# Computing five of six modulation sublayers of a two-block transformer kernel on VectorE instead of TensorE

## The chip, the core and the metric

The kernel runs on one core of a Trainium2 chip. The metric is the device time of one launch in microseconds (us). The core has a matrix engine (TensorE, PE in the profile, with its weight loads as PEld), three engines for elementwise work (VectorE, DVE; ScalarE, ACT; GpSimd, POOL), and a queue that issues most transfers (SyncE, SP). Each engine works through its own instructions in order and waits for the others by semaphores.

## The reference, cut to what matters

Two blocks follow one another, each with two layers, on 256 tokens of 1024 channels in float32. The first block has four branches. The second has, in each layer, three sublayers: a feed-forward network (FFN), an attention, a second FFN. Each sublayer normalises its rows and modulates them, by a shift, a scale and a gate that come from two conditioning vectors and one large matrix per layer:

```python
c_act = jax.nn.silu(c)
cc_act = jax.nn.silu(c_ctx)
for layer in range(DEPTH):
    mod = (c_act @ w_mod[layer] + b_mod[layer]).reshape(b, 1, N_MOD, D_MODEL)
    mod_c = (cc_act @ w_mod[layer] + b_mod[layer]).reshape(N_MOD, D_MODEL)
    ...
    shift, scale, gate = mods_of(m, sub)
    y = swiglu(modulate(rms_norm(h, g_pre[sub]), shift, scale), w1, w2)
    return h + MACARON_WEIGHT * gate * rms_norm(y, g_post[sub])
```

`w_mod` is 1024 x 9216 a layer: 3072 columns for each of the 2 x 3 sublayers. Only two rows are multiplied with it.

## The kernel before, in words

All large products are float32 products in three passes. A load (`wload`) brings 1024 columns of weights (128 x 1024, 512 KB) into a buffer `wr` (four of them); ScalarE writes the high part `wh` (L177), VectorE the low part `wl` (L178), three buffers each; TensorE then multiplies high by high, high by low and low by high (L169). In the FFNs and in the attention's projections one load feeds 24 matmuls of 512 columns, alternately into the PSUM banks `ac` and `rw`.

Every `wload` ends with `tick()`, which takes a step of the generators in `self.bg`. So small chains of work are spread between the large products. The modulation is such a generator, `mods`. Its step loads one `wr` tile of `w_mod` and issues two matmuls into the bank `md`, with the conditioning vectors as the stationary part (32 columns wide, so that a product fills one of four column groups of the array). Four steps make a half row; then ScalarE copies `md` out (L1173), two transfers bring it to DRAM, and after six half rows the sums are made, written to DRAM and read back (L1175 to L1199). A sublayer takes 24 steps with products and 9 others. Sublayer (0,0) is made in layer 1 of the first block, a step a tick; the other five run in the second block, a step every second tick (`MODS_TICKS`). `pre`, which opens the next sublayer, waits for its modulation.

Inside the attention, `scores` makes the softmax of two heads (scores in `ac` and `rw`, then VectorE L1529 to L1536, ScalarE, VectorE L1552) and `values` transposes the result and multiplies it with v. There are no weight loads there, so ticks are called by hand: `HEAD_TICKS` = 6 at a pair of heads of the first stream and 2 of the second. `HEADS_AHEAD` = (0, 1) says how many pairs may have their values still to come. A scheduler then sets the final order of the instructions on each engine.

Of the kernel before, what the change touches and what calls it, by code (L numbers as in the profile page):

```python
# [9 lines left out]
F32 = mybir.dt.float32  # L10
# [3 lines left out]
AF = mybir.ActivationFunctionType  # L14
# [5 lines left out]
L = 2  # L20
D = 1024
# [31 lines left out]
RWKV_STEPS = ((2, 1), (2, 1))           # by layer and duo  # L53
RWKV_GAPS = (2, 3, 3, 2, 1, 4)
CONV_STEPS, CONV_GAP, XQ_GAP, MLA_GAPS = 3, 2, 1, (2, 1)
MODS_TICKS = 2                          # ticks a step
HEAD_TICKS = (6, 2)                     # ticks at a pair of heads, by stream
HEADS_AHEAD = (0, 1)                    # pairs whose values wait, by stream
EVS = 5                                 # buffers
COLS = ((0, 1), (1, 2), (3, 2), (5, 2), (7, 1))     # row tiles that are transposed at a time  # L60
# [99 lines left out]
class Build:  # L160
# [6 lines left out]
    # -- building stones --  # L167
# [6 lines left out]
    def split(self, h, l, src, eng=None):  # L174
        """src = h + l exactly, h and l with the 12 significant bits of float32r"""
        nc = self.nc
        nc.scalar.copy(h, src)  # L177
        (eng or nc.vector).tensor_tensor(out=l, in0=src, in1=h.bitcast(F32), op=ALU.subtract)  # L178
# [15 lines left out]
    def gemm(self, out, sa, sb, KT):  # L194
        """out = sum over k of a^T b, three float32r passes; sa(k), sb(k) give (high, low)"""
# [7 lines left out]
    def rsqrt(self, out, in_, n):  # L203
        """out = in_ ** -0.5 (exact to float32 rounding), [p, n]"""
        p = in_.shape[0]
        self.nc.gpsimd.tensor_tensor(out=out, in0=in_, in1=self.mhalf[:p, :n], op=ALU.pow)  # L206
# [9 lines left out]
    def tick(self):  # L216
        """a step of the work that is spread over the stream of weights"""
# [17 lines left out]
    # -- the whole --  # L235
    def build(self):
        nc, tc, ap = self.nc, self.tc, self.ap
        with ExitStack() as st:
# [15 lines left out]
            # what the end of the first block needs on the one side, the rest of it and then the second on the other  # L254
# [7 lines left out]
    # ================= first block =================  # L262
    def first(self, fin, st):
# [3 lines left out]
        self.ts = fin.enter_context(tc.tile_pool(name="ts", bufs=4))     # a few columns  # L267
        p1 = self.p1 = pool("p1", 1)
        self.f4 = fin.enter_context(tc.tile_pool(name="f4", bufs=7))     # [128, 1024]
# [9 lines left out]
        self.t1 = pool("t1", 2)     # [128, 256] scratch  # L279
        self.t2 = pool("t2", 2)     # [128, 512] scratch  # L280
        self.d2 = pool("d2", 16)    # [128, 512], four heads of the recurrence
        self.d4 = pool("d4", 5)     # [128, 1024]
        self.rp = pool("rp", 1)     # its diagonal blocks
# [5 lines left out]
    def trig(self):  # L289
        """cos and sin of positions * inv_freq, [token, tile, 16]"""  # L290
# [27 lines left out]
        # the quotient may be off by one either way  # L318
# [63 lines left out]
    def params(self, l):  # L382
        """the small weights of a layer"""
# [4 lines left out]
        # halves and the like, worked out on the chip  # L388
# [21 lines left out]
    def wtile(self, ps):  # L410
        """the next 128 columns of w_in"""
# [8 lines left out]
    def move(self, ps, h, lo, kt, k0, K, lhs, n=512):  # L420
        """ps += rows k0.. of the weights (n columns each), streamed; lhs(k) the stationary parts"""
# [7 lines left out]
    def memkv(self, l):  # L429
        """k^T [d, head, m] and v [m, (head d)] of the memory tokens"""  # L430
# [29 lines left out]
    def gated(self, n):  # L460
        """silu(gate) times the branch, in two parts: the operands of the output projection"""
# [16 lines left out]
    # -- RWKV --  # L478
    def shift(self, p, mu, omu, out):
        """out = (1 - mu) * p + mu * p_prev, tokens along the free dimension"""  # L480
# [47 lines left out]
        # decay and learning rate  # L528
# [26 lines left out]
        # kk = k * k_k, normalised per head  # L555
# [24 lines left out]
        # scaled operands  # L580
# [18 lines left out]
        # inverses of the 16x16 diagonal blocks, row after row: a row of a block goes to the partitions of its block  # L599
# [26 lines left out]
        # by token  # L626
# [15 lines left out]
        # bonus  # L642
# [12 lines left out]
        # blocks of 32, then of 64  # L655
# [29 lines left out]
        # u = ta S + c0 for the state S of a chunk, and S' = e (m S + cs)  # L685
# [46 lines left out]
        # the rows: rk v + rb u, and r S  # L732
# [9 lines left out]
        # there is no state before the first chunk  # L742
# [19 lines left out]
        # group norm over a head, and the bonus  # L762
# [27 lines left out]
    # -- convolution --  # L790
# [31 lines left out]
    def norm_stats(self, src, eps, n=1):  # L822
        """mean and (variance + eps) ** -0.5 of the rows; src a list of [128, <=512]"""
# [11 lines left out]
    def conv_norm(self):  # L835
        """layer norm over the channels, then silu: self.cx becomes 2 silu(.)"""
# [24 lines left out]
    # -- attention over the memory --  # L861
# [835 lines left out]
```

## Time and profile before

| what | us |
|---|---|
| median of three runs (2756.73, 2757.94, 2766.02) | 2757.94 |
| profiled execution, span from first to last instruction | 2758.4 |
| PE busy in it | 2691.4 |
| DVE busy | 1539.3 |
| ACT busy | 1145.3 |
| POOL busy | 219.5 |

The profiled execution is known by its span; nothing else of it is recorded, and the span stands 0.46 us above the median of the runs. The second block begins at about 868 us of the span. Its stages are, in order: FFN and attention of layer 0, FFN, FFN of layer 1 (from about 1990), attention (from about 2385), last FFN. The two stretches in which the attention makes its scores and values are 1413.5 to 1511 and 2454.5 to 2511; the text calls them the score stages.

### The profile page before, as it was taken

The numbers are of one execution on the slowest core, as the hardware profiler recorded it, in microseconds if no ns is written. First come the engines' busy times: TensorE is split into PE (matmuls) and PEld (weight loads), VectorE is DVE, ScalarE is ACT, GpSimd is POOL, SyncE is SP. The second block draws the span as 40 slices with busy tenths as digits, with TensorE's granted clock in tenths as the row PEclk, the third lists the DMA queues.
The fourth block names the chain that finished last, engine by engine and source line by source line (L and its number), as shares of the span: only waits on it lengthen the run. The fifth ranks groups of instructions, "written<-read, shape, count | busy, mean of one in ns | idle before, by whom it ended". The sixth has DMA issues, their size and how long they took to land.

```text
span 2758.4 us, 43028 instructions
## 1 busy us (share of the span) xinstructions
PE 2691.4 (98%) x17138; PEld 2183.3 (79%) x17138; DVE 1539.3 (56%) x2646; ACT 1145.3 (42%) x1964; POOL 219.5 (8%) x240
## 2 busy tenths in 40 slices
PE   8999999999999999999999999999999999999999
PEld 7888998787999777777755777777777777765897
DVE  7997667897666533345635442335533334744656
ACT  5465455445545322234436422224422224535445
POOL 1121110112011000000102000000000000110000
PEclk9999999999999999999999999999999999999999
DMA  6344466546366534434433344444444343434565
GB/s 204 95 129 131 150 199 212 161 141 183 116 185 204 168 119 130 128 111 127 120 108 111 115 119 127 124 121 118 123 130 122 117 131 116 131 123 135 168 183 151
DMA packets 134906, 385.07 MB, mean 140 GB/s; under 512 B 38481, under 2 KB 42385, under 8 KB 134577
## 3 DMA queue, kind: packets, MB, share of 16 engines
q1 hardware_dynamic: 121216, 379.25, 45.7%
q10 hardware_dynamic: 13488, 3.07, 0.5%
q8 instruction: 135, 2.21, 0.3%
q14 instruction: 67, 0.54, 0.1%
HBM read 379.43 MB, written 2.83 MB: 139 GB/s over the span
## 4 chain that ended last, share of the span: by engine, by line
PE 86%; DVE 8%; ACT 2%; issue 2%; DMA 1%; POOL 1%; ACTq 0%; DVEq 0%; SPq 0%; POOLq 0%
PE ac L169 42%; PE rw L169 27%; PE sm L169 10%; PE md L169 5%; PE sm L172 2%; DVE wl L178 2%; DVE br L817 2%; DMA wr<-in_win 1%; DVE br L1352 0%; ACT wh L177 0%; PE rw L172 0%; POOL rso L206 0%; POOL rs L206 0%; DVE u L1345 0%; DVE u L1263 0%
## 5 line engine op out<-in xcount | busy, mean ns | idle before, releaser
L178 DVE TENSOR_TENSOR wl<-wr,wh 128x1024 fp32r<-128x1024 f32 (+2 forms) x547 | 699.5, 1280 | 507.9 <-ACT wh L177 506.1
L177 ACT CAST wh<-wr 128x1024 fp32r<-128x1024 f32 (+2 forms) x547 | 568.2, 1039 | 953.6 <-PE ac L169 439.2
L169 PE MATMUL rw<-blk,wh 128*128 128x512 f32 (+1 forms) x1712 | 461.6, 354 | 1.3 <-DVE blk L1282 1.1
L169 PE MATMUL ac<-blk,wh 128*128 128x512 f32 (+1 forms) x1728 | 460.8, 352 | 0.0
L169 PE MATMUL ac<-xth,wh 128*128 128x256 f32 x1248 | 357.7, 287 | 5.7 <-ACT wh L177 5.2
L169 PEld LDWEIGHTS rw<-blk,wh 128*128 128x128 f32 x1712 | 302.4, 191 | 71.2 <-ACT wh L177 27.7
L169 PEld LDWEIGHTS ac<-blk,wh 128*128 128x128 f32 x1728 | 305.4, 190 | 58.5 <-ACT wh L177 14.3
L169 PE MATMUL ac<-xth,wl 128*128 128x256 f32 x1248 | 350.0, 281 | 1.2 <-DVE wl L178 1.2
L169 PE MATMUL ac<-xtl,wh 128*128 128x256 f32 x1248 | 349.9, 281 | 0.1
L169 PE MATMUL rw<-blk,wl 128*128 128x512 f32 (+1 forms) x856 | 301.0, 352 | 4.2 <-DVE wl L178 4.2
L169 PE MATMUL ac<-blk,wl 128*128 128x512 f32 (+1 forms) x864 | 301.9, 349 | 1.8 <-DVE wl L178 1.8
L169 PEld LDWEIGHTS ac<-xth,wh 128*128 128x128 f32 x1248 | 236.2, 189 | 22.2 <-issue 10.7
L169 PEld LDWEIGHTS ac<-xth,wl 128*128 128x128 f32 x1248 | 236.1, 189 | 3.8 <-DVE wl L178 2.2
L169 PEld LDWEIGHTS ac<-xtl,wh 128*128 128x128 f32 x1248 | 236.4, 190 | 2.5 <-issue 1.6
L178 DVE TENSOR_TENSOR al<-blk,ah 128x512 fp32r<-128x512 f32 (+1 forms) x170 | 104.9, 621 | 146.8 <-ACT ah L177 146.6
L169 PEld LDWEIGHTS rw<-blk,wl 128*128 128x128 f32 x856 | 163.1, 191 | 26.8 <-DVE wl L178 4.4
L169 PEld LDWEIGHTS ac<-blk,wl 128*128 128x128 f32 x864 | 164.1, 190 | 23.4 <-DVE wl L178 2.2
L177 ACT CAST ah<-blk 128x512 fp32r<-128x512 f32 (+1 forms) x170 | 95.4, 564 | 201.1 <-PE rw L169 102.6
L169 PE MATMUL md<-wr,cs 128*32 128x512 f32 x576 | 158.0, 612 | 3.7 <-DMA wr<-in_wmod 2.2
L1396 DVE SCALAR_TENSOR_TENSOR blk<-u,rw 128x512 f32<-128x512 f32 (+1 forms) x66 | 39.5, 598 | 160.9 <-PE rw L169 160.8
L206 POOL TENSOR_TENSOR rso<-rso,mhalf 128x1 f32<-128x1 f32 x20 | 11.0, 551 | 1420.7 <-DVE rso L1347 1420.7
L169 PE MATMUL ac<-f,wh 128*128 128x256 f32 x640 | 117.0, 282 | 0.0
(417 smaller groups left out, 4112.1 us busy)
## 6 DMA issues: line engine op xcount, KB each, us to landing
wr<-in_w SPq DMA_DIRECT2D x264, 512.0 KB
wr<-in_win SPq DMA_DIRECT2D x187, 512.0 KB
wr<-in_wmod SPq DMA_DIRECT2D x144, 512.0 KB
wr<-in_wo SPq DMA_DIRECT2D x32, 512.0 KB
wr<-in_wout SPq DMA_DIRECT2D x32, 512.0 KB
wr<-in_wkv SPq DMA_DIRECT2D x16, 512.0 KB
gate<-gd SPq DMA_DIRECT2D x10, 512.0 KB
blk<-in_rpb SPq DMA_DIRECT2D x48, 64.0 KB
```

The costliest lines, as they stand in the source:

```text
L169: self.nc.tensor.matmul(out, a, b, start=start, stop=stop, skip_group_check=True)
L172: self.nc.tensor.transpose(out, a, self.ident[:n, :n])
L177: nc.scalar.copy(h, src)
L178: (eng or nc.vector).tensor_tensor(out=l, in0=src, in1=h.bitcast(F32), op=ALU.subtract)
L206: self.nc.gpsimd.tensor_tensor(out=out, in0=in_, in1=self.mhalf[:p, :n], op=ALU.pow)
L817: V.scalar_tensor_tensor(out=acc, in0=hp[:, j : j + 256], scalar=w(j), in1=acc, op0=ALU.mult, op1=ALU.add)
L1396: V.scalar_tensor_tensor(out=a(u // 2), in0=t, scalar=0.5, in1=pu, op0=ALU.mult, op1=ALU.mult)
```

## The change

The modulation of the five sublayers after the first is computed by VectorE. `wmodT` holds the transposed matrix: a tile has 128 output channels in its partitions and the 1024 inputs along them. `cr` holds silu of the two conditioning vectors, copied to all partitions. One instruction per tile and vector (`tensor_tensor_reduce`, L1188, "ISA" in the order, with a second one that reads the accumulator) multiplies and sums. A group of 128 channels is one tile and two such products (one where the second vector isn't needed): 120 groups, 208 products. The group's next tile is fetched after its products; the gaps between groups are 2, 2 and 1 ticks, a step a tick. Shift and scale then lie by channel without a way through DRAM; the gate is transposed once and written to DRAM.

The ticks by hand in the attention go, and `HEADS_AHEAD` becomes (1, 1). Sublayer (0,0) still uses `mods`, but now loads two tiles in one step and issues their four matmuls, one to each column group, in the next. `kernel` sets a smaller DMA scratch, and `second` calls `c_rows`. Comments are left out of the diff.

```diff
-MODS_TICKS = 2                          # ticks a step
-HEAD_TICKS = (6, 2)                     # ticks at a pair of heads, by stream
-HEADS_AHEAD = (0, 1)                    # pairs whose values wait, by stream
+MODS_GAPS = (2, 2, 1)
+HEADS_AHEAD = (1, 1)
...
+    def c_rows(self):
+        nc = self.nc
+        self.cr = self.p2.tile([128, 2, 1024], F32, name="cr")
+        self.prod = self.p2.tile([128, 1024], F32, name="prod")
+        for r in range(2):
+            nc.sync.dma_start(out=self.cr[:, r], in_=self.ap["cR"][r].partition_broadcast(128))
+            nc.scalar.activation(self.prod, self.cr[:, r], AF.Tanh, scale=0.5)
+            nc.vector.scalar_tensor_tensor(out=self.cr[:, r], in0=self.prod, scalar=1.0, in1=self.cr[:, r], op0=ALU.add,
+                                           op1=ALU.mult)
+            nc.vector.tensor_scalar(out=self.cr[:, r], in0=self.cr[:, r], scalar1=0.5, scalar2=None, op0=ALU.mult)
+    def mods_rows(self, *which):
...
+        todo = [(l, sub, g) for l, sub in which for g in range(24)]
+        raw = fetch(*todo[0])
+        yield
+        for n, (l, sub, g) in enumerate(todo):
...
+            for r in range(2 if both(g) else 1):
+                V.tensor_tensor_reduce(out=self.prod, in0=raw, in1=self.cr[:, r], scale=1.0, scalar=0.0, op0=ALU.mult,
+                                       op1=ALU.add, accum_out=m[:, g, r : r + 1])
+            if n + 1 < len(todo):
+                raw = fetch(*todo[n + 1])
...
+            for _ in range(MODS_GAPS[n % len(MODS_GAPS)]):
+                yield
...
     def mods(self, *which):
-                for i in range(4):
+                for i in range(0, 4, 2):
                     u = 4 * blk + i
-                    raw = self.wr.tile([128, 1024], F32, name="wr")
-                    nc.sync.dma_start(out=raw, in_=ap["wmod"][l, :, 1024 * u : 1024 * u + 1024])
-                    for k in range(2):
-                        kk = 2 * i + k
-                        g = 32 * (kk % 4)
-                        self.mm(ps[g : g + 32], self.cs[:, kk], raw[:, 512 * k : 512 * k + 512], kk < 4, kk >= 4)
+                    raw = [self.wr.tile([128, 1024], F32, name="wr") for _ in range(2)]
+                    for j in range(2):
+                        nc.sync.dma_start(out=raw[j], in_=ap["wmod"][l, :, 1024 * (u + j) : 1024 * (u + j) + 1024])
+                    yield
+                    for k in range(4):
+                        self.mm(ps[32 * k : 32 * k + 32], self.cs[:, 2 * i + k],
+                                raw[k // 2][:, 512 * (k % 2) : 512 * (k % 2) + 512], i == 0, i == 2)
                     yield
...
             if l == 0:
-                self.bg.append((self.mods((0, 1), (0, 2), (1, 0), (1, 1), (1, 2)), -MODS_TICKS))
+                self.c_rows()
+                self.bg.append((self.mods_rows((0, 1), (0, 2), (1, 0), (1, 1), (1, 2)), 1))
...
                     P = self.scores(s, kind, heads, q, k, nab, sink)
-                    for _ in range(HEAD_TICKS[s]):
-                        self.tick()
...
-    nc = _bacc.Bacc("TRN2", target_bir_lowering=False, num_devices=1)
+    nc = _bacc.Bacc("TRN2", target_bir_lowering=False, num_devices=1, dynamic_dma_scratch_size=1024)
```

What this does to the order shows best at three places. First TensorE at the start of the score stage of layer 0 (`rw`, `ac` with two `blk`: scores; `ident`: transposes; `md`: modulation). Before:

```order
L169 MATMUL rw_14839<-blk_14046,blk_14047 128x512 x2
L169 MATMUL ac_14840<-blk_14046,blk_14047 128x512 x2
L169 MATMUL md_14863<-wr_14864,cs_6333 32x512 x2
L169 MATMUL md_14863<-wr_14868,cs_6333 32x512 x2
L169 MATMUL md_14863<-wr_14913,cs_6333 32x512 x2
L169 MATMUL md_14863<-wr_14917,cs_6333 32x512 x2
L169 MATMUL rw_14872<-blk_14046,blk_14047 128x512 x2
L169 MATMUL ac_14873<-blk_14046,blk_14047 128x512 x2
```

And in the change:

```order
L168 MATMUL rw_14888<-blk_14083,blk_14084 128x512 x2
L168 MATMUL ac_14889<-blk_14083,blk_14084 128x512 x2
L171 MATMUL md_15792<-ident_69,gt_14835 16x128
L168 MATMUL rw_14908<-blk_14083,blk_14084 128x512 x2
L168 MATMUL ac_14909<-blk_14083,blk_14084 128x512 x2
```

The products of the modulation are gone; one transpose of the gate is left, and the scores follow one another.

Second, VectorE in the first product of layer 0's FFN (`wl`: low parts of the next weights; the two lines with `u2`: the activation; `prod`: the new products). Before:

```order
L178 TENSOR_TENSOR wl_11891<-wr_11888,wh_11890 128x1024
L178 TENSOR_TENSOR wl_11922<-wr_11919,wh_11921 128x1024
L1395 SCALAR_TENSOR_TENSOR u2_11884<-u2_11884,ac_11823 128x512
L1396 SCALAR_TENSOR_TENSOR blk_11347<-u2_11884,rw_11859 128x512
L178 TENSOR_TENSOR wl_11961<-wr_11958,wh_11960 128x1024
```

And in the change:

```order
L177 TENSOR_TENSOR wl_11940<-wr_11937,wh_11939 128x1024
L1455 SCALAR_TENSOR_TENSOR u2_11902<-u2_11902,ac_11842 128x512
L1188 ISA prod_11348,mm_11374<-wr_12015,cr_11347 128x1024
L1188 ISA mm_11374 128x1
L1188 ISA prod_11348,mm_11374<-wr_12015,cr_11347 128x1024
L1188 ISA mm_11374 128x1
L1456 SCALAR_TENSOR_TENSOR blk_11357<-u2_11902,rw_11877 128x512
L177 TENSOR_TENSOR wl_11979<-wr_11976,wh_11978 128x1024
```

The products stand between the low parts of the weights, so a late product makes the next `wl` late.

Third, SyncE's queue at the start of the second block's first FFN (`w1`: weights; `cb`: constants, 1248 KB; `cR`: the conditioning rows, `gate`: the gate rows, 512 KB each). Before:

```order
L185 DMA wr_11607<-in_w1 128x1024
L185 DMA wr_11638<-in_w1 128x1024
L1221 DMA cb_11345<-in_cb 128x2496
L1166 DMA wr_11644<-in_wmod 128x1024
L1292 DMA gate_13011<-gd00_6342 128x1024 x2
L185 DMA wr_11677<-in_w1 128x1024
```

And in the change:

```order
L184 DMA wr_11583<-in_w1 128x1024
L1173 DMA wr_11591<-in_wmodT 128x1024
L1280 DMA cb_11345<-in_cb 128x2496
L1160 DMA cr_11347<-in_cR 128x1024 x2
L1352 DMA gate_13048<-gd00_6342 128x1024 x2
L184 DMA wr_11622<-in_w1 128x1024
```

Before, the weights of the fifth and sixth unit (11607 and 11638) went ahead of `cb`. Now those of the fifth (11622) come after `cb`, the new rows and the gate.

## Rows read from the trace of the kernel before

**Rows 1.** The page: busy time of each engine, share of the span, instructions.

```profile
PE 2691.4 (98%) x17138; PEld 2183.3 (79%) x17138; DVE 1539.3 (56%) x2646; ACT 1145.3 (42%) x1964; POOL 219.5 (8%) x240
```

**Rows 2.** The page: chain that ended last, its shares by engine and line.

```profile
PE ac L169 42%; PE rw L169 27%; PE sm L169 10%; PE md L169 5%; PE sm L172 2%; DVE wl L178 2%; DVE br L817 2%; DMA wr<-in_win 1%; DVE br L1352 0%; ACT wh L177 0%; PE rw L172 0%; POOL rso L206 0%; POOL rs L206 0%; DVE u L1345 0%; DVE u L1263 0%
```

**Rows 3.** That chain in order of time, FFN of layer 0: start, duration, what.

```profile
948.92 5.44 PE ac L169 x24
954.36 0.98 PE md L169 x4
955.34 5.67 PE rw L169 x24
...
1020.27 5.44 PE ac L169 x24
1025.71 5.44 PE rw L169 x24
```

**Rows 4.** Windows, tile md alone: stretch, length; PE, PEld, DVE, ACT; clock, DMA.

```profile
505.00:700.00 195.00, 27.58 (x97) 3.85 (x97) 0.19 (x1) 3.52 (x6) 1.00 0.54 163
868.00:1413.50 545.50, 34.95 (x129) 4.87 (x129) 0.19 (x1) 4.63 (x8) 0.99 0.43 130
1413.50:1511.00 97.50, 17.77 (x73) 2.61 (x73) 0.19 (x1) 2.36 (x4) 0.93 0.39 119
1511.00:2454.50 943.50, 63.48 (x226) 8.86 (x226) 0.39 (x2) 8.13 (x14) 1.00 0.41 122
2454.50:2511.00 56.50, 15.43 (x56) 1.97 (x56) 0.00 (x0) 1.78 (x3) 0.94 0.36 113
```

**Rows 5.** Windows, all work: PE, PEld, DVE, ACT, POOL busy (records); clock, DMA, GB/s.

```profile
511.00:630.00 119.00, 116.83 (x1216) 90.68 (x1214) 110.82 (x255) 49.35 (x100) 19.73 (x24) 1.00 0.51 156
925.00:1190.00 265.00, 265.00 (x1172) 204.44 (x1171) 92.74 (x105) 67.10 (x83) 0.00 (x0) 1.00 0.42 124
1190.00:1330.00 140.00, 138.68 (x673) 108.65 (x671) 74.77 (x107) 62.38 (x108) 9.87 (x9) 1.00 0.42 122
1413.50:1511.00 97.50, 94.96 (x441) 45.74 (x441) 56.08 (x225) 53.29 (x146) 19.40 (x15) 0.93 0.39 119
1850.00:1990.00 140.00, 138.49 (x672) 109.33 (x671) 74.47 (x111) 62.05 (x107) 5.25 (x8) 1.00 0.40 115
2240.00:2385.00 145.00, 143.69 (x685) 113.11 (x684) 75.10 (x113) 63.25 (x110) 5.35 (x9) 1.00 0.42 116
2454.50:2511.00 56.50, 54.14 (x235) 21.44 (x236) 32.00 (x140) 27.34 (x72) 8.31 (x5) 0.94 0.36 113
```

**Rows 6.** Timeline of PE in layer 0's score stage: start, us, instruction.

```profile
1436.10 1.06 PE L169 MATMUL md<-wr,cs 128*32 128x512 f32 x8
1437.10 0.65 PE L169 MATMUL sm<-pt,gate 128*64 128x256 f32 x4
```

**Rows 7.** VectorE's groups by line and shape: busy, mean ns | idle before.

```profile
L178 DVE TENSOR_TENSOR wl<-wr,wh 128x1024 fp32r<-128x1024 f32 x535 | 691.2, 1293 | 501.7 <-ACT wh L177 499.9
L1529 DVE DVE_READ_ACCUMULATOR2_ANT hm<- 128x1 f32 x48 | 6.7, 139 | 0.0
L1529 DVE CUSTOM_DVE_ANT_0 ac<-ac,blk 128x256 f32<-128x256 f32 x12 | 5.1, 426 | 26.0 <-PE ac L169 26.0
L1120 DVE SCALAR_TENSOR_TENSOR br<-br,mvar,d 128x1024 f32<-128x1024 f32 x2 | 2.5, 1274 | 0.0
```

**Rows 8.** What PE waited for from 2335 to 2400: total, times, longest.

```profile
PE rw L169 <- DVE wl L178: 4.2, 1, 4.2
```

**Rows 9.** SyncE's timeline and the windows, 917 to 930.

```profile
917.45 0.33 SPq L1221 DMA_DIRECT2D cb<-in_cb  x1
...
920.00:930.00 10.00, 9.35 (x76) 9.01 (x76) 6.78 (x14) 6.34 (x11) 0.00 (x0) 1.00 0.66 240
```

**Rows 10.** The chain in order of time: fifth unit's matmuls; a weight load.

```profile
936.83 5.44 PE ac L169 x24
...
647.47 5.45 DMA wr<-in_win
```

More of the change, by code (lines that the diff above doesn't have):

```diff
@@ new lines, in mods_rows, with fetch @@
+    def mods_rows(self, *which):
+        nc, ap = self.nc, self.ap
+        V = nc.vector
+        def fetch(l, sub, g):
+            raw = self.wr.tile([128, 1024], F32, name="wr")
+            nc.sync.dma_start(out=raw, in_=ap["wmodT"][l, sub, :, 1024 * g : 1024 * g + 1024])
+            return raw
+        todo = [(l, sub, g) for l, sub in which for g in range(24)]
+        raw = fetch(*todo[0])
+        yield
+        for n, (l, sub, g) in enumerate(todo):
+            if g == 0:
+                both = (lambda g: l < L - 1 or sub == 0 or (sub == 1 and g < 16))
+                m = self.us.tile([128, 24, 2], F32, name="mm", bufs=2)
+                pm = self.us.tile([128, 40], F32, name="pm", bufs=2)
+                nc.sync.dma_start(out=pm, in_=ap["pmodT"][l, sub])
+                nc.gpsimd.memset(m, 0.0)
+            for r in range(2 if both(g) else 1):
[3 more added lines that the diff above has]
+                raw = fetch(*todo[n + 1])
+            if g == 23:
+                col = lambda a: pm[:, a : a + 8].unsqueeze(2).to_broadcast([128, 8, 2])
+                mc = self.mc[l]
+                V.tensor_tensor(out=m, in0=m, in1=pm[:, 0:24].unsqueeze(2).to_broadcast([128, 24, 2]), op=ALU.add)
+                V.tensor_copy(mc[:, 2 * sub], m[:, 0:8])
+                V.scalar_tensor_tensor(out=mc[:, 2 * sub + 1], in0=m[:, 8:16], scalar=1.0, in1=col(24), op0=ALU.add,
+                                       op1=ALU.mult)
+                gt = self.us.tile([128, 2, 8], F32, name="gt", bufs=2)
+                V.scalar_tensor_tensor(out=gt.rearrange("p r k -> p k r"), in0=m[:, 16:24],
+                                       scalar=D**0.5 * (1.0 if sub == 1 else 0.5), in1=col(32), op0=ALU.mult, op1=ALU.mult)
+                yield
+                ps = self.md.tile([128, 512], F32, name="md")
+                self.tr(ps[:16, 0:128], gt.rearrange("p r k -> p (r k)"))
+                gr = self.us.tile([16, 128], F32, name="gr", bufs=2)
+                V.tensor_copy(gr, ps[:16, 0:128])
+                nc.scalar.dma_start(out=self.gd[l, sub][2].rearrange("r (k c) -> (r k) c", c=128), in_=gr)
+                self.modded.add((l, sub))
+            for _ in range(MODS_GAPS[n % len(MODS_GAPS)]):
+                yield
@@ L1162, in mods @@
                 ps = self.md.tile([128, 512], F32, name="md")
-                for i in range(4):
+                for i in range(0, 4, 2):
                     u = 4 * blk + i
-                    raw = self.wr.tile([128, 1024], F32, name="wr")
-                    nc.sync.dma_start(out=raw, in_=ap["wmod"][l, :, 1024 * u : 1024 * u + 1024])
-                    for k in range(2):
-                        kk = 2 * i + k
-                        g = 32 * (kk % 4)
-                        self.mm(ps[g : g + 32], self.cs[:, kk], raw[:, 512 * k : 512 * k + 512], kk < 4, kk >= 4)
+                    raw = [self.wr.tile([128, 1024], F32, name="wr") for _ in range(2)]
+                    for j in range(2):
+                        nc.sync.dma_start(out=raw[j], in_=ap["wmod"][l, :, 1024 * (u + j) : 1024 * (u + j) + 1024])
+                    yield
+                    for k in range(4):
+                        self.mm(ps[32 * k : 32 * k + 32], self.cs[:, 2 * i + k],
+                                raw[k // 2][:, 512 * (k % 2) : 512 * (k % 2) + 512], i == 0, i == 2)
                     yield
@@ L1653, in pack @@
     out["cT"] = np.stack([i["c_2"].reshape(8, 128).T, i["c_ctx_2"].reshape(8, 128).T], 2)
-    out["wmod"] = np.stack([_move(i["w_mod_2"][l], 2) for l in range(L)])
+    out["cR"] = np.stack([i["c_2"].reshape(D), i["c_ctx_2"].reshape(D)])
+    out["wmod"] = _move(i["w_mod_2"][0][:, : 3 * D], 2)[None]
+    out["wmodT"] = i["w_mod_2"].transpose(0, 2, 1).reshape(L, 3, 24, 128, D).transpose(0, 1, 3, 2, 4).reshape(L, 3, 128, -1)
+    cols = [i["b_mod_2"].reshape(L, 3, 24, 128)] + [i[n].reshape(L, 3, 8, 128) for n in ("g_pre_2", "g_post_2")]
+    out["pmodT"] = np.concatenate(cols, 2).transpose(0, 1, 3, 2)
     rows = [i["b_mod_2"].reshape(L, 3, 3, 64, 16)] + [i[n].reshape(L, 3, 1, 64, 16) for n in ("g_pre_2", "g_post_2")]
```

## Prediction

> **What bounds the kernel now.** I read the busy times first: TensorE is busy 98% of the span, VectorE 56%, ScalarE 42% [rows 1]. The chain of work that ended last says the same: most of it is matmuls, and 5% of the span is the modulation's, on the path itself [rows 2]. So time that leaves TensorE is gained, as long as nothing else ends later in its place. The question is what the modulation's matmuls take out of TensorE's time, and whether VectorE, which takes the work over, has room where it gets it.
>
> How dear a step is shows in the chain in order of time [rows 3]. In the FFN a unit of 24 matmuls takes 5.44 us when the next follows at once. Where a step of the modulation stands between, its two matmuls (four records) take 0.98 us, and the 24 that follow take 5.67. A step costs 0.98 + 0.23 = **1.21 us**.
>
> How many steps there are, and where, is counted by windows of the tile `md` [rows 4]. Each step leaves four records; what is over is a transpose (one, one, one, two and none in the five stretches). So there are 24 steps in the first block (96 records), 32 + 56 = 88 in the second block between large products (128 and 224), and 18 + 14 = 32 in the two score stages (72 and 56). 88 + 32 = 120 is the five sublayers of 24.
>
> **The change part by part, against the profiled span of 2758.4 us** (the median of the runs is 0.46 lower, so the sum stands for either).
>
> *The 88 steps between large products.* They lie on TensorE's path with no idle time beside them: in 925 to 1190 it is busy 265.00 of 265.00 us [rows 5]. They go whole: 88 x 1.21 = **106.5 us gained**.
>
> *The 32 steps in the score stages* take 17.77 + 15.43 = 33.2 us of TensorE [rows 4]. Here they were filler: scores wait for a softmax on VectorE and ScalarE, and the modulation ran meanwhile. Bounds: all 33.2 come back, or none, if the softmax is late by as much. TensorE without them has 94.96 - 17.77 = 77.2 us of work in the first stage, VectorE 56.1, ScalarE 53.3 [rows 5]; so no other engine is full, but each step of the chain must be in time. One more pair of heads may now run ahead in the first stream, which helps. I take half, **16.6 gained**.
>
> *The 24 steps of sublayer (0,0)* become 12 with four matmuls. In the score stage four matmuls (eight records) took 1437.10 - 1436.10 = 1.00 us [rows 6], as two do in the FFN, so the column groups work at the same time. That is 12 x 1.21 = 14.5 us of TensorE. But here VectorE is busy 110.8 of 119 us [rows 5], and two of the four load buffers are now held for a tick more. Bounds: 14.5 gained, or 5 lost (about one weight load, 5.45 us [rows 10], that comes late). I take **7 gained**.
>
> *What VectorE gets.* 208 products of 128x1024 from two float32 operands in SBUF. No such one is in the trace: the same instruction on 128x256 took 426 ns, with its accumulator read of 139 ns behind it [rows 7]. Four times that is 1.70 us; a two-operand instruction of 128x1024 on SBUF took 1274 ns, another 1293 [rows 7]. The longer shape shows that part of the 426 ns is fixed, so I take 1.28 + 0.14 = 1.42 us, and 2.84 a group of two. 24 groups are spread over 41 ticks (24 x 5/3, and one) of 5.44 us: 68 of 223 us, 31% of VectorE's time. In 925 to 1190 it was 35% busy, so 66% to 70% now: nothing is lost. In the stretches with the second product of an FFN and the change of sublayer it was 74.8 of 140, 74.5 of 140 and 75.1 of 145 us [rows 5]. With about 10 us of modulation gone from each, that is 57%, so 88% now. It fits on average, but at the change of sublayer the normalisation, the transposed rows and the next weights all queue on VectorE, and TensorE has waited there before: 4.2 us for a `wl` [rows 8]. Each product that stands in that queue delays it by 1.42 us. Bounds over the four changes while the products run: nothing, or two groups each, 4 x 2 x 2.84 = 23 us. I take the middle, **11 lost**.
>
> *The start of the second block.* Ahead of the fifth unit's weights there now stand 1248 KB and four times 512 KB, 3.25 MB. At the 240 GB/s of that stretch they need 13.5 us from the issue of `cb` at 917.45 [rows 9]; the weights themselves 2 more, then a `wl` of 1.3 and the cast before it of about as much (an estimate from the same `wl`). That is 936, and TensorE takes the fifth unit at 936.83 [rows 10]. Just covered; but ScalarE and VectorE also make `cr` in their queues there. Bounds: nothing, or 13.5 us if `cb` goes out that much later. I take **4 lost**. The last transposes of the gate and the sums of a sublayer (some 128x48 and less) I cost at nothing: they hide beside the matmuls with VectorE at 70%, and would cost a few tenths each if it were full.
>
> Sum: 106.5 + 16.6 + 7 - 11 - 4 = 115 us. 2758.4 - 115 = **2643 us**.
>
> **The rivals.**
>
> *VectorE's products run at half rate.* Then 1.28 becomes 2.56, a group 5.4 us, the load 58% instead of 31%. In the first product of an FFN it still fits (38% of the shortened stretch and 58%), in the three stretches named it comes to 115%: 20 us too much in each, 60 instead of the 11 lost, **2692 us**. Against it: the two-operand instructions of rows 7 with both operands in SBUF are not slow. For it: they don't sum. [...] The scalar_tensor_tensor of rows 7, without a sum, doesn't show it; no run here shows the shape with a sum on two SBUF operands.
>
> [...]
>
> *The other side: VectorE waits in its queue for the transposed tiles.* A product waits for its transfer, and every `wl` behind it waits too. A weight load took 5.45 us [rows 10]; the fetch is issued one or two ticks ahead (5.4 or 10.9 us), if a buffer is free. With a wait of w a group, VectorE's time per tick is 0.38 x 5.44 + 0.585 x (2.84 + w) in some 130 ticks and 0.575 x 5.44 + the same in some 75. The excess over 5.44 comes to 120 w - 271 us, against 130 gained: it decides from **w = 3.3 us**. With w = 4 it is 2758.4 - 130 + 209 = **2837 us**. Against it: a buffer is now freed by VectorE, not by TensorE some units later, so loads go out earlier than before.
>
> *All goes well:* the score stages give 33.2, (0,0) gives 14.5, nothing is lost: 154 us, **2604 us**.
>
> That the change doesn't do what it says is excluded by the order: the matmuls are gone from TensorE's row.
>
> **How the numbers follow.** Forecast 60% (its own range, with some of the bounds either way, 2618 to 2672), all well 12%, half rate 12%, low clock 11%, waiting in the queue 5%. The range of eight in ten takes the forecast, the good case to its number, and half rate to 10 us above its own: 2604 to 2702; low clock and the queue, 16% together, stay outside. A measurement of this kernel can tell about 0.3% (8 us) from no change. Slower by more than that is the queue's case, less a bit for a small w: 4%; within it 2%; faster 94%.
>
> **What would show it.** Right: the modulation's group is gone from the chain in the second block, units of 24 matmuls follow each other every 5.44 us, VectorE has 208 products of about 1.28 us, and the score stages take some 8 us less each. Wrong: products of over 2 us; TensorE waiting for `wl` by more than 20 us in all; a granted clock well below 0.9 in the score stages; VectorE idle before the products, released by a transfer.

## The result, and the profile after

| | before | changed |
|---|---|---|
| median of four runs, us | 2761.8 | 2675.6 |
| runs, us | 2756.73 to 2766.02 | 2674.33 to 2684.92 |
| span of the profiled execution, us | 2758.4 | 2674.9 |

The ratio is 0.9699, with a 95% interval of 0.9677 to 0.9722. The forecast was 2643 us, 115 us less than before. The profiles lie 83.5 us apart, the medians 86. So the direction and the main mechanism held, and some 30 us of the gain are missing.

The busy times of the changed kernel, which answer to [rows 1]:

```profile
PE 2581.7 (97%) x16658; PEld 2173.0 (81%) x16658; DVE 1769.6 (66%) x3066; ACT 1133.5 (42%) x1936; POOL 228.1 (9%) x245
```

TensorE has 110 us less to do and is still the engine that is busy nearly all the time. VectorE has 230 us more. (The groups below add to more than that, since the busy time counts records that overlap once.)

VectorE's groups by line and shape, columns as in [rows 7]:

```profile
L177 DVE TENSOR_TENSOR wl<-wr,wh 128x1024 fp32r<-128x1024 f32 x535 | 689.1, 1289 | 255.7 <-ACT wh L176 254.2
L1188 DVE CUSTOM_DVE_ANT_0 prod<-wr,cr 128x1024 f32<-128x1024 f32 x208 | 254.4, 1223 | 259.7 <-DMA wr<-in_wmodT 258.5
...
L1188 DVE DVE_READ_ACCUMULATOR2_ANT mm<- 128x1 f32 x208 | 17.2, 83 | 0.0
...
L1323 DVE TENSOR_SCALAR u<-br,rs 128x1024 f32<-128x1024 f32 x12 | 9.0, 753 | 7.8 <-POOL rs L205 7.8
```

A product takes 1223 ns and its read 83. The read's record begins before that of the product ends, as VectorE's timeline shows for one group (start, us, instruction, idle time before):

```profile
1020.18 1.23 DVE L1188 CUSTOM_DVE_ANT_0 prod<-wr,cr 128x1024 f32<-128x1024 f32 x1 [1.94 <-DMA wr<-in_wmodT]
1021.33 0.09 DVE L1188 DVE_READ_ACCUMULATOR2_ANT mm<- 128x1 f32 x1
1021.45 1.23 DVE L1188 CUSTOM_DVE_ANT_0 prod<-wr,cr 128x1024 f32<-128x1024 f32 x1
```

The next product starts 1.27 us after the one before it, where the forecast took 1.42 for a product with its read. The idle time on the second row of the groups is new: VectorE stood 258.5 us in its queue until a transposed tile had landed.

The tile `md` alone, in two of the stretches that answer to [rows 4] (columns as there):

```profile
505.00:700.00 195.00, 17.52 (x97) 2.59 (x97) 0.18 (x1) 3.49 (x6) 0.99 0.51 162
912.00:1414.00 502.00, 0.55 (x2) 0.17 (x2) 0.55 (x2) 0.00 (x0) 0.98 0.49 152
```

The matmuls of five sublayers are gone, and the four-matmul steps of (0,0) take 10 us less of TensorE.

The surprise is in TensorE's timeline, in the first product of layer 0's first FFN: the first row of three units of 24 matmuls that follow one another (start, us, instruction):

```profile
1004.17 0.63 PE L168 MATMUL rw<-blk,wh 128*128 128x512 f32 x2
...
1009.77 0.63 PE L168 MATMUL ac<-blk,wh 128*128 128x512 f32 x2
...
1015.37 0.63 PE L168 MATMUL rw<-blk,wh 128*128 128x512 f32 x2
```

A unit takes 5.60 us, with TensorE busy throughout (16.80 of 16.80 us from 1004.17 on). Before it was 5.44 [rows 3]. And in the last FFN, which has no modulation in either kernel and whose first product has matmuls of 256 columns, a unit takes 2.72 us now. The chain in order of time of the kernel before has 2.88 there, that of the changed kernel 2.72:

```profile
2570.19 2.88 PE ac L169 x24
2573.07 2.88 PE rw L169 x24
```

```profile
2520.65 2.72 PE ac L168 x24
2523.37 2.72 PE rw L168 x24
```

Wide units (512 columns) became 3% slower and narrow ones (256 columns) 6% faster, at a granted clock of 1.00 in all four.

To see where the time went, the span is cut at the first inverse square root on GpSimd of each change of sublayer (`rstd` at the start of the second block, `rso` after that). The table also has runs that follow; each stage is in us, from one profile.

| stage | before | changed | e5 | e4 | e6 | e9 | e11 | e12 |
|---|---|---|---|---|---|---|---|---|
| up to the second block | 907.3 | 912.0 | 904.7 | 907.7 | 907.8 | 910.5 | 911.2 | 907.8 |
| FFN 1 | 386.7 | 369.1 | 369.6 | 367.1 | 365.1 | 365.7 | 358.5 | 370.0 |
| attention 1 | 265.6 | 256.7 | 249.9 | 251.1 | 249.1 | 247.0 | 245.0 | 251.7 |
| FFN 2 | 396.9 | 381.4 | 382.7 | 375.7 | 381.0 | 374.5 | 368.6 | 373.1 |
| FFN 3 | 397.3 | 377.2 | 377.3 | 376.0 | 370.6 | 370.5 | 368.8 | 369.5 |
| attention 2 | 199.0 | 179.9 | 178.8 | 181.7 | 181.6 | 186.8 | 186.9 | 178.5 |
| last FFN | 197.6 | 190.7 | 190.7 | 190.7 | 197.5 | 195.2 | 197.0 | 194.7 |

The rest is 8.0 us in each.

### The profile page after: what moved, and what is told of

It is laid out like the page before. It is cut to its first block, busy times and chain, and to the rows that moved or that the text cites. A ratio compares the mean times of both kernels' runs of the same rounds, so it can differ in the third digit from the quotient of the medians.

```text
span 2674.9 us, 42375 instructions
## 1 busy us (share of the span) xinstructions
PE 2581.7 (97%) x16658; PEld 2173.0 (81%) x16658; DVE 1769.6 (66%) x3066; ACT 1133.5 (42%) x1936; POOL 228.1 (9%) x245
## 3 DMA queue, kind: packets, MB, share of 16 engines
q8 instruction: 131, 2.15, 0.3%
## 5 line engine op out<-in xcount | busy, mean ns | idle before, releaser
L1188 DVE CUSTOM_DVE_ANT_0 prod<-wr,cr 128x1024 f32<-128x1024 f32 x208 | 254.4, 1223 | 259.7 <-DMA wr<-in_wmodT 258.5
L816 DVE SCALAR_TENSOR_TENSOR br<-hp,pv,br 128x256 f32<-128x256 f32 x240 | 114.1, 512 | 0.9
```

What stands on the lines that cost most here:

```text
L816: V.scalar_tensor_tensor(out=acc, in0=hp[:, j : j + 256], scalar=w(j), in1=acc, op0=ALU.mult, op1=ALU.add)
L1188: V.tensor_tensor_reduce(out=self.prod, in0=raw, in1=self.cr[:, r], scale=1.0, scalar=0.0, op0=ALU.mult, op1=ALU.add, accum_out=m[:, g, r ...
```

## The experiments

**Theory.** The change moves tiles in SBUF, the memory on the chip that holds the operands. It puts small tiles into the pool `us` and so shifts `blk`, which is allocated after it; by the built program's allocation `blk` starts 128 bytes over a multiple of 256 before, and 64 over in the changed kernel (below for short: 128 over, 64 over). `wh` and `wl` stand 128 over in both. `blk` is the moving operand (the first one behind the arrow in a row; the second, `wh` or `wl`, is the stationary one) of 3192 matmuls of 512 columns, 133 units. At 0.16 us each they cost 21 us, and the last FFN gives 7 back. **Rival:** the products on VectorE, or their transfers, slow the matmuls. A second rival came up later: before, the modulation's own matmuls broke TensorE's stream and kept it at the faster pace.

### e1: `blk` at a multiple of 128

```diff
     def junk(self):
-        return self.us.tile([128, 512], BF16, name="junk", bufs=1)
+        return self.us.tile([128, 544], BF16, name="junk", bufs=1)[:, :512]
```

> The changed kernel with a scratch tile 64 bytes larger, so that the tiles `blk` stand at multiples of 128 bytes again, as before; nothing else. In the changed kernel they stand 64 bytes off, and a unit of 24 matmuls of 512 columns takes 5.60 us in the first products, where before it took 5.44; in the last FFN, which has no modulation in either kernel, a unit of 24 matmuls of 256 columns takes 2.72 where before it took 2.88. Theory (the address sets the pace): units go back to 5.44, some 3100 matmuls by 6.7 ns or 21 us gained, and to 2.88 in the last FFN, 7 us lost; with small terms about 2660 us. Rival (VectorE's products or their transfers slow the matmuls): units stay at 5.60 and 2.72, 2676 us.

Measured: ratio to before 0.9725 (0.9694 to 0.9755), 2678.34 us. The last FFN went back most of the way, 196.2 us in place of 190.7. The wide units hardly moved; TensorE's timeline, three unit starts:

```profile
1002.33 0.62 PE L168 MATMUL rw<-blk,wh 128*128 128x512 f32 x2
...
1007.90 0.63 PE L168 MATMUL ac<-blk,wh 128*128 128x512 f32 x2
...
1013.48 0.62 PE L168 MATMUL rw<-blk,wh 128*128 128x512 f32 x2
```

5.57 and 5.58 us. So an address does matter, but 128 was not the period: `blk` stood at a multiple of 256 here, and before it had stood 128 over one.

### e2: the kernel before, with `blk` 64 over

The same edit in the kernel before.

> The kernel before with a scratch tile 64 bytes larger, so that `blk` stands 64 bytes off a multiple of 128 bytes, as in the changed kernel; the modulation stays on TensorE. Theory (address): units of 512 columns take 5.60 without any product on VectorE, units of 256 columns in the last FFN 2.72; 21 us lost and 7 gained, about 2772 to 2776 us. Rival (VectorE's products are the cause): no change, 2762 us and units of 5.44.

Measured: ratio 1.0037 (1.0020 to 1.0053), 2767.72 us against 2755.15 of the runs beside it: 12.6 slower. The chain in order of time, first FFN and last FFN:

```profile
1097.83 5.60 PE ac L169 x24
1103.42 0.98 PE md L169 x4
1104.41 5.79 PE rw L169 x24
1110.20 5.60 PE ac L169 x24
...
2587.05 2.72 PE ac L169 x24
```

This is the changed kernel's pace, wide and narrow, with no product on VectorE and with the modulation's matmuls in between. That rules out the rival: moving `blk` does it, at a cost near the 14 us net that were worked out. (The edit moves some scratch tiles with it, `u2`, `u4`, `ss` and `xc`; these matmuls don't read them.)

### e3: the last FFN's operands moved by 16 columns

e1, and in the last FFN the operands `hh` and `hl` lie 16 columns further in their rows, so 64 bytes over:

```diff
+        self.o = 16 if (l, sub) == (1, 2) else 0
...
-            h = self.hh[:, k : k + m, 256 * s : 256 * s + 256]
+            sl = slice(256 * s + self.o, 256 * s + 256 + self.o)
+            h = self.hh[:, k : k + m, sl]
...
```

> As the run with `blk` at multiples of 128 bytes, and in the last FFN, whose operands fill 256 of 512 columns of a row, these are put 16 columns (64 bytes) further. Theory (address): 5.44 in the wide units and 2.72 in the last FFN, about 2653 us, better than both kernels. Rival (some other property of the program sets the pace of the last FFN): 2.88 there and 2660 us, or no change at all and 2676 us.

Measured: 0.9703 (0.9677 to 0.9730), 2672.69 us. The last FFN took 190.7 us with units of 2.72 again, where e1 had 196.2. Here the operand's address did it; e7 shows that it isn't all. The wide units stayed near 5.58, so there was no gain in all.

### e4: no products

```diff
-        raw = fetch(*todo[0])
...
-            for r in range(2 if both(g) else 1):
-                V.tensor_tensor_reduce(out=self.prod, in0=raw, in1=self.cr[:, r], scale=1.0, scalar=0.0, op0=ALU.mult,
-                                       op1=ALU.add, accum_out=m[:, g, r : r + 1])
-            if n + 1 < len(todo):
-                raw = fetch(*todo[n + 1])
```

> The changed kernel without the 208 products and the 120 transfers of the transposed matrix: the sums of the modulation of five sublayers are left out. What it costs VectorE and the queue is the difference to the changed kernel. Theory (address sets the pace, VectorE has room): units stay at 5.60, and 3 to 12 us are gained at the changes of sublayer, 2664 to 2673 us. Rival (the products slow the matmuls by traffic): units go to 5.44 and some 25 us or more are gained, 2650 us or less.

Measured: 0.9654 (0.9629 to 0.9678). Against the changed kernel's 0.9694 in another group of runs (e5) that is 0.4%, 11 us; the two intervals just overlap. Wide units stayed at 5.60, again against the rival. By stage (table, against e5), products and transfers cost 2.5 us in FFN 1, 7.0 in FFN 2, 1.3 in FFN 3: 11 us as well.

### e5: the changed kernel again

> The changed kernel itself, beside the others of this group on one chip, and with a profile of its own. Both theories: a ratio to the kernel before of 0.970 within 0.003, units of 5.60 in the wide first products and 2.72 in the last FFN. What it tells beside that: whether the time at the low clock in the two score stages (34.1 and 13.7 us in the first profile) belongs to the kernel or changes from run to run; by the runs so far (10.2 and 30.7 with the last FFN's operands moved) it changes, and with it 7 to 10 us of a stage.

Measured: 0.9694 (0.9662 to 0.9725). The units of the first products are as in the first profile. The second product of FFN 1 is not: two rows of TensorE's timeline that are 12 matmuls apart, first profile and this one:

```profile
1224.79 0.40 PE L168 MATMUL ac<-wh,ah 128*128 128x512 f32 x1
...
1227.59 0.40 PE L168 MATMUL rw<-wh,ah 128*128 128x512 f32 x1
```

```profile
1217.82 0.39 PE L168 MATMUL ac<-wh,ah 128*128 128x512 f32 x1
...
1220.57 0.39 PE L168 MATMUL rw<-wh,ah 128*128 128x512 f32 x1
```

That is 233 ns a matmul against 229, in the same program at the same addresses, the slower one at a granted clock of 1.00 (first profile, 1224.79 to 1227.99); e4, without products, shows the 233 too. So a pace can change between executions for a reason that no run here shows.

The first score stage took 102.5 us, not 109.3. Windows from the first scores to the last values of both score stages (columns as in [rows 5]), first profile and this one:

```profile
1397.80:1507.10 109.30, 103.68 (x454) 57.71 (x452) 59.62 (x243) 57.65 (x165) 21.69 (x18) 0.84 0.05 17
2392.60:2459.40 66.80, 62.53 (x285) 33.74 (x283) 38.64 (x153) 36.70 (x90) 9.65 (x6) 0.90 0.05 17
```

```profile
1391.00:1493.50 102.50, 96.83 (x454) 54.72 (x452) 59.25 (x243) 57.53 (x165) 21.52 (x18) 0.92 0.06 18
2379.20:2446.00 66.80, 62.35 (x283) 33.77 (x283) 38.70 (x153) 36.70 (x90) 9.65 (x6) 0.90 0.05 17
```

The same 454 records took 103.68 us at a mean granted clock of 0.84, and 96.83 at 0.92. In windows of 1 us the first profile's clock is 0.50 from 1402 to 1435 and, but for the two windows at its ends (0.74 and 0.69), 1.00 in the rest of the stage: 34.1 us at the low clock of 0.50. In its second score stage 0.50 lasts 13.7 us (2398.2 to 2411.8). If the clock in e5 is 0.50 or 1.00 too, 0.92 is 16 us (an estimate from the mean). In e3 the two stages, otherwise the same, came the other way round:

```profile
1396.60:1496.60 100.00, 94.32 (x453) 53.71 (x452) 59.40 (x243) 57.50 (x165) 21.56 (x18) 0.95 0.06 19
2381.90:2456.10 74.20, 69.53 (x283) 36.56 (x283) 38.83 (x153) 37.04 (x90) 9.67 (x6) 0.79 0.05 15
```

So a score stage differs by 7 to 9 us from execution to execution, and the longer one has the lower mean clock each time. The kernel before does the same: its first score stage, in its own profile and in that of e2:

```profile
1412.90:1526.90 114.00, 111.41 (x526) 56.90 (x524) 61.23 (x245) 61.67 (x171) 22.41 (x18) 0.94 0.34 103
```

```profile
1423.70:1532.20 108.50, 105.88 (x525) 54.48 (x524) 61.13 (x245) 61.78 (x171) 22.43 (x18) 1.00 0.36 109
```

### e6: `blk` as before

```diff
-        return self.us.tile([128, 512], BF16, name="junk", bufs=1)
+        return self.us.tile([128, 608], BF16, name="junk", bufs=1)[:, :512]
```

> The changed kernel with a scratch tile 192 bytes larger, so that `blk` stands as it did before against multiples of 256 (and of 1024) bytes, 128 over; `wh` and `wl` do so in all kernels. With `blk` at a multiple of 256 the wide units took 5.58, 64 over 5.60, in the kernel before (128 over) 5.44. Theory A (address alone): units of 5.44 throughout and 2.88 in the last FFN: some 3100 matmuls by 6.7 ns or 21 us less, 7 us more, so 14 us faster than the changed kernel. Theory B (before, the modulation's own matmuls broke the stream every two units and so kept it at the fast pace): units of about 5.58 and 2.88, 7 us slower than the changed kernel.

Measured: 0.9665 (0.9642 to 0.9688), 2665.9 us beside 2670.5 of e5. The 14 us of theory A didn't come: the intervals overlap. TensorE's timeline, three unit starts:

```profile
1003.78 0.62 PE L168 MATMUL ac<-blk,wh 128*128 128x512 f32 x2
...
1009.22 0.62 PE L168 MATMUL rw<-blk,wh 128*128 128x512 f32 x2
...
1014.66 0.62 PE L168 MATMUL ac<-blk,wh 128*128 128x512 f32 x2
```

Yet the units take 5.44 us, without anything in between: theory A has their pace right, and theory B is out. FFN 3 gained the 6.7 us that its wide matmuls are worth, and the last FFN lost 6.8. But FFN 2 gained 1.7 only. What TensorE waited for there, in total, times, longest:

```profile
PE rw L168 <- DVE blk L1456: 3.4, 1, 3.4
PE sm L171 <- DVE u L1323: 1.9, 3, 1.2
PE ac L168 <- DVE wl L177: 1.2, 1, 1.2
PE ac L168 <- DVE blk L1342: 0.8, 1, 0.8
```

The four longest are all on VectorE. Its products in that stage, by the groups, the stage's row of the windows, and that row in e5:

```profile
L1188 DVE CUSTOM_DVE_ANT_0 prod<-wr,cr 128x1024 f32<-128x1024 f32 x74 | 90.4, 1222 | 105.9 <-DMA wr<-in_wmodT 105.5
...
1522.00:1903.00 381.00, 371.81 (x1696) 307.48 (x1695) 241.83 (x355) 123.38 (x181) 9.57 (x9) 0.99 0.47 148
```

```profile
1524.10:1906.80 382.70, 375.83 (x1696) 305.31 (x1695) 242.74 (x355) 123.51 (x181) 9.59 (x10) 1.00 0.48 147
```

VectorE was busy 241.83 of 381.00 us and stood another 105.5 in its queue, waiting for tiles. That is 347 of 381, with little room for faster units. TensorE's idle time grew from 6.9 us in e5 to 9.2. But its busy time fell by 4.0 us only, where 41 units make 6.6, and the mean granted clock is 0.99 where e5 has 1.00. So of the 5 us that are missing about half are waits, and about half go with the low clock. e9 tests whether VectorE's load is behind it.

### e7: the same, with the last FFN's operands 64 over

e6, with e3's edit at 48 columns in place of 16.

> As the run with `blk` as before, and the operands of the last FFN put 48 columns (192 bytes) further in their rows, so that they stand 64 over a multiple of 256, as in the changed kernel. Theory A: 5.44 in the wide units and 2.72 in the last FFN, 21 us faster than the changed kernel, the fastest of all. Theory B: no difference to the changed kernel within 3 us.

Measured: 0.9658 (0.9632 to 0.9684). Wide units took 5.44. The last FFN's took neither value; its chain in order of time:

```profile
2521.22 2.83 PE rw L168 x24
2524.04 2.83 PE ac L168 x24
```

By the allocation the operands stand at the very addresses that gave 2.72 in the changed kernel and in e3. So the moving operand's address doesn't settle the narrow units alone; what else does stays open.

### e8: single loads in sublayer (0,0)

The method `mods` of the kernel before, in the changed kernel.

> The changed kernel with the old step for sublayer (0,0): one load and two matmuls in one step, 24 steps where it has 12 with four matmuls. If the pairing is worth the 7 us of the forecast, this is 7 us slower than the changed kernel. Rival: VectorE sets the pace of that stage (busy 93% before), so the matmuls saved are worth nothing, and the times agree within 3 us.

Measured: 0.9686 (0.9660 to 0.9711) beside 0.9694. The windows of that stage, between the two `rstd` that enclose it, first e8, then e5:

```profile
452.70:731.10 278.40, 270.66 (x2547) 227.07 (x2546) 221.88 (x477) 134.95 (x263) 45.58 (x55) 0.99 0.54 164
```

```profile
453.10:731.40 278.30, 262.91 (x2548) 227.28 (x2547) 220.16 (x477) 133.77 (x263) 47.90 (x55) 0.99 0.52 163
```

The pairing takes 7.75 us from TensorE and nothing from the stage: all of it became idle time of TensorE. So the rival's times came out. That VectorE alone sets the pace is not shown: the longest waits of TensorE that e5 has there and e8 hasn't are 2.0 us for ScalarE (`mq`) and 1.0 each for VectorE (`d`, `wl`).

### e9: a gap of two ticks in layer 1

e6, with e3's edit (now 192 over a multiple of 256), and:

```diff
-            for _ in range(MODS_GAPS[n % len(MODS_GAPS)]):
+            for _ in range(MODS_GAPS[n % len(MODS_GAPS)] if l == 0 else 2):
```

> As the run with `blk` as before, with a gap of two ticks after every group of layer 1's modulation (2, 2, 1 before), so that the FFN after the attention has some 10 groups fewer products on VectorE and the next FFN more; and the last FFN's operands 16 columns (64 bytes) further, which is 192 over a multiple of 256, an address not seen yet. Theory (VectorE's load holds the FFN after the attention, which took 381.0 us where the next one took 370.6): that FFN takes about 376, the next one not over 372. Rival (something else than the products makes that FFN longer): 381 and 371. Last FFN: 2.72 a unit if 64 and 192 are alike, else 2.88. In all 5 to 12 us faster than the run with `blk` as before.

Measured: 0.9636 (0.9593 to 0.9680), 2655.23 us. FFN 2 took 374.5 us in place of 381.0, and FFN 3 the same 370.5; VectorE had 66 products in FFN 2 in place of 74, TensorE was idle for 4.8 us in place of 9.2, and its mean granted clock was 1.00. e12, with the same gaps, has 373.1, and e7, with the old ones, 381.8. So the rate at which groups come is what held FFN 2. The narrow units took 2.83 (195.2 us).

### e10: HEADS_AHEAD back at (0, 1)

> The changed kernel with HEADS_AHEAD back at (0, 1): the first stream's pairs have no values waiting. Theory (the pair ahead is what fills TensorE's wait for the softmax now that the modulation's matmuls don't): the first score stage takes 115 us or more where it took 100 to 109, and the whole is 8 to 20 us slower than the changed kernel. Rival (the scheduler's order or the second stream fills it anyway): the stages as before within their changes from run to run, no difference in all.

Measured: 0.9727 (0.9698 to 0.9757) beside 0.9694, the intervals overlapping. The 0.3% between them, 9 us, would fit the theory's 8 to 20, but its reason isn't borne out: the first score stage took 108.0 us, not 115. The windows of both stages:

```profile
1399.60:1507.60 108.00, 102.61 (x452) 56.62 (x452) 60.42 (x243) 57.95 (x165) 21.60 (x18) 0.86 0.06 17
2393.40:2467.60 74.20, 70.86 (x284) 37.36 (x284) 38.27 (x153) 37.01 (x90) 10.12 (x6) 0.77 0.05 15
```

Both lengths are those of the kernel with (1, 1) at the same clock (109.30 at 0.84, 74.20 at 0.79). Whether the older setting makes the low clock longer, one profile can't tell.

### e11: no products, fast units

e4 with e6's edit, and `ah` and `al` 64 bytes further (a larger tile `prod` ahead of them), at 128 over a multiple of 256 in place of 64:

```diff
-        self.prod = self.p2.tile([128, 1024], F32, name="prod")
+        self.prod = self.p2.tile([128, 1040], F32, name="prod")[:, :1024]
```

> The changed kernel without products and transfers of the transposed matrix (the sums of the modulation of five sublayers are left out), with `blk` as before, and with `ah` and `al` 64 bytes further, at 128 over a multiple of 256. Theory (with fast units VectorE's products are what still costs): against the run with `blk` as before the FFN after the attention falls from 381 to 369 us, the first from 365 to about 361, the next hardly (370.6 to 369.5); 14 us less than the run without products at the old address. The second products of the FFNs go from 228.9 to 226.7 ns a matmul if the stationary operand's address counts too. Rival (the FFN after the attention is longer for another reason): 378 or more there.

Measured: 0.9579 (0.9551 to 0.9608), 2642.8 us. FFN 2 fell to 368.6, FFN 1 to 358.5, FFN 3 to 368.8. Between e6 and this lie 0.86% or 24 us; some 4 of them are worth `ah`'s address (1776 matmuls by 2.3 ns, next run), so on fast units the products and their transfers cost about 20 us, where on slow units they cost 11.

### e12: the edits together

e9 and the larger tile `prod` of e11; everything is computed.

> The run with the gaps of two ticks, and `ah` and `al` 64 bytes further, at 128 over a multiple of 256, as in the run without products on fast units. Theory (each address counts by itself): the second products of the FFNs go from 228.9 to 226.7 ns a matmul, in each FFN some 528 matmuls by 2.2 ns or 1.2 us, 4 to 5 us in all; wide units stay at 5.44; a ratio of about 0.962 to the kernel before, the fastest that computes everything. Rival (the second products were fast only because VectorE was idle): they stay at 228.9, ratio 0.964.

Measured: **0.9615** (0.9588 to 0.9642), 2651.49 us, clear of the changed kernel's 0.9694 (0.9662 to 0.9725). The end of the chain shows 120 matmuls of the last second product, in the changed kernel and in this one:

```profile
2637.90 27.48 PE sm L168 x120
```

```profile
2616.41 27.21 PE sm L168 x120
```

That is 229.0 and 226.7 ns a matmul. In the last FFN neither kernel has products left, so this alone doesn't answer the rival. FFN 2 has them, and TensorE's timeline there has two rows, 12 matmuls apart:

```profile
1859.65 0.39 PE L168 MATMUL ac<-wh,ah 128*128 128x512 f32 x1
...
1862.37 0.39 PE L168 MATMUL ac<-wh,ah 128*128 128x512 f32 x1
```

Those are 226.7 ns a matmul while VectorE has its products (e9 takes 2.75 us for 12 there, 229.2): the stationary operand's address counts too. By the medians e12 is 0.2% or 6 us ahead of e9, but their intervals overlap. FFN 1 took 370.0 us here and 365.7 in e9: TensorE waited 4.5 us once for `blk` from VectorE (3.2 in e9, 5.0 in e7 with its 372.4), and the mean granted clock was 0.99 where e9 has 1.00. That stage comes out differently by a few us.

## Why the prediction was right, and where it was not

The measured 2675.6 us lies inside the range of eight in ten, 2604 to 2702, but above the 2618 to 2672 that the prediction gives the forecast itself. The mechanism is the forecast's: time that left TensorE between the large products was gained. That the number stayed inside is in part luck. The address of `blk`, for which there was no term, cost some 21 us and gave 7 back in the last FFN, and the part of the range that holds 2675.6 had been put in for products at half rate, which didn't come. Of the signs of being wrong two showed: a granted clock of 0.84 in the first score stage, and VectorE idle until a transfer lands. Of the signs of being right, units of 5.44 us did not show.

The forecast by stage, from its own terms (25, 9, 24, 24 and 6 of the 88 steps by the records of `md`, 2.75 us lost at each of four changes), beside the two profiles:

| stage | forecast gain | measured | missing |
|---|---|---|---|
| up to the second block | 7 | -4.7 | 11.7 |
| FFN 1 | 23.5 | 17.6 | 5.9 |
| attention 1 | 17.0 | 8.9 | 8.1 |
| FFN 2 | 26.3 | 15.5 | 10.8 |
| FFN 3 | 26.3 | 20.1 | 6.2 |
| attention 2 | 15.0 | 19.1 | -4.1 |
| last FFN | 0 | 6.9 | -6.9 |
| sum | 115.1 | 83.4 | 31.7 |

FFN 2's 10.8 are about the 6.6 of its 41 units at 0.16 us and the 4.3 by which products and transfers cost more there (7.0 by e4) than the 2.75. Most of the 8.1 in attention 1 belongs to this one profile: e5 took 249.9 us there, 1.3 from the forecast's 248.6.

- **The 88 steps: the mechanism held, the price was off, and this is the term that was furthest off.** A pair of units with its step took 12.09 us before (5.44 + 0.98 + 5.67). The forecast let 10.88 be left of it; the profile has 11.20. So a step gave 0.89 us, not 1.21: 28 us less if all 88 stood between two such units; counted by the 133 units that `blk` feeds, it is 21. The 5.44 was a duration at one place in memory, carried over to a program that allocates differently. e2 and e6 show it in both directions for the units. For the whole, e6 won only 5 us back. In e6, with `blk` as before, FFN 3 gained 26.7 us: the forecast's 26.3.
- **The last FFN** gained 6.9 us by the same shift. The forecast had no term for it.
- **Sublayer (0,0): 7 forecast, nothing measured** (e8). The forecast named VectorE's 110.8 of 119 us and still took 7 from between its bounds; the row should have decided. Nor did four matmuls go at the price of two: by the tile `md` a step took 17.52 / 12 = 1.46 us where one of two took 27.58 / 24 = 1.15. The other 4.7 us up to the second block are no cost of the change that these profiles show: the changed kernel's second profile reached that point at 904.7, ahead of before's 907.3, and the kernel before in e2 at 910.9.
- **The score stages: 16.6 forecast.** From the first scores to the last values, 114.0 and 79.1 us became 109.3 and 66.8, 17.0 less; in e5 102.5 and 66.8, 23.8 less. Against e2's profile of the kernel before, 108.5 and 78.8, it is 11.2 and 18.0. So the half was a fair choice, but these profiles can't tell it to better than some 6 us.
- **VectorE's price** held: 1.27 us from product to product where 1.42 was taken. The half-rate rival (2.56 us) is out; no run shows such a rate. In this trace the sum halves nothing: 1223 ns with it, 1289 for `wl` of the same size without. Both take longer than the instruction with one tensor operand, 753 ns (L1323).
- **At the changes and at the start 15 us lost** were forecast; e4 puts it at 11 for products and transfers, e11 at about 20 when the units are fast. FFN 2 took 7.0 of the 11, more than its share.
- **VectorE waiting in its queue** was given 5% as what decides, from 3.3 us a group. The wait is there: 258.5 us over 120 groups, 2.15 each, and 105.5 us in FFN 2 of e6 alone. It stayed below the point from which it decides. In e6's FFN 2 it stands beside the gain that didn't come. Whether an earlier fetch would remove it was not tried.
- **The low clock**, as staying through both score stages, was given 11%. No run shows that: the two stages of the first profile, 176.1 us of 2674.9, would by themselves bring the mean clock to 0.967 at 0.50 (an estimate), and the lowest of any run is 0.978. It did come in part: 34.1 and 13.7 us at 0.50 in the score stages of the first profile, means of 0.84 and 0.90, where the kernel before had 0.94 and 0.94. By the stages above it is worth up to 9 us a stage (an estimate) and differs in each execution. The mean over a whole execution is lower too: 0.979 to 0.984 in the four runs of the changed kernel, 0.989 to 0.995 in the kernel before beside e5. In e5's four runs 0.987 goes with 2663.4 us and 0.978 with 2682.9. By that rate the 0.008 between the two kernels' means in that group is worth some 17 us (an estimate). That may be part of the half of 33.2 us that the score stages didn't give back; no run held the clock fixed, so this isn't shown.

## What to carry to other kernels

A change that adds or drops a tile moves the tiles allocated after it, and here a matmul's pace changed with where its operands start: by 3% between 128 and 64 bytes over a multiple of 256. So compare a unit of untouched work first, in a stage that the edit doesn't concern; if it differs, look at addresses before looking for contention, and pad a tile to test it. And time that leaves the engine that works nearly all the time can be worth nothing: 7.75 us of TensorE's were, in a stage where VectorE was busy 93% of a long stretch.

## What the runs showed of the hardware that was not expected

TensorE's time for 24 matmuls, by where the moving operand `blk` starts over a multiple of 256 bytes (`wh` at 128 over in all):

| `blk` | 512 columns, us | 256 columns in the last FFN, us |
|---|---|---|
| 128 | 5.44 (before, e6, e7, e9, e12) | 2.88 (before, e6) |
| 64 | 5.60 (changed, e2, e4, e5) | 2.72 (changed, e2, e3); 2.83 (e7) |
| 0 | 5.58 (e1, e3) | 2.85 (e1) |
| 192 | not run | 2.83 (e9, e12) |

Of the four places, the best for wide matmuls is the worst for narrow ones. With the stationary operand `ah` at 64 over a matmul of 512 columns took 229.0 ns, at 128 over 226.7; but at 64 over it also took 233.3 in some executions (FFN 1 of the first profile and of e4). Why the address does this, whether its period is 256 or more, and what else sets the narrow units (e7) and the second products stays open. The trace shows the pace and no cause for it.
